# A fourth tile for the transposed values in the RWKV stage of a two-block fp32 network, paid for with unused DMA scratch

## The chip, the cores and the metric

The kernel runs as one launch on one core of a Trainium2 chip. The time is device microseconds of that core, the median of several executions. Smaller is better.

## What is computed

The program is a chain of two blocks over 256 tokens of width 1024, all in float32. The first has two layers, each a gated feed-forward, a mixer with a convolution and a linear recurrence, and another feed-forward. The second has an RWKV layer and a differential attention layer, over a context of 256 tokens and the 256 tokens themselves. The change lies in the RWKV layer. Cut to that, the reference is:

```python
def wkv_scan(r, w, k, v, kk, a, s0, reverse):
    def step(S, inp):
        r_t, w_t, k_t, v_t, kk_t, a_t = inp
        sa = jnp.einsum("bhvk,bhk->bhv", S, kk_t)
        S = (S * w_t[:, :, None, :] - sa[..., None] * (kk_t * a_t)[:, :, None, :]
             + v_t[..., None] * k_t[:, :, None, :])
        return S, jnp.einsum("bhvk,bhk->bhv", S, r_t)
    s_fin, o = lax.scan(step, s0, xs, reverse=reverse)

def rwkv7_mixer(...):            # 16 heads of 64
    oc_f, sc_f = scan_direction(con, 0, s0, False)   # context, forwards
    oc_b, sc_b = scan_direction(con, 1, s0, True)    # context, backwards
    ol_f, _ = scan_direction(lat, 0, sc_f, False)    # tokens, from the context's state
    ol_b, _ = scan_direction(lat, 1, sc_b, True)
    y = rwkv7_readout(ol_f + ol_b, lat, ...)
```

## The kernel before

A Python program writes out every engine's instructions in one fixed order. It keeps a clock of its own for each engine, with an assumed cost for each operation, and holds many generators ("chains"). At each matmul of the large products it lets those chains emit their next few instructions whose inputs and buffers its clock takes as ready. So a buffer that comes free earlier in that clock moves instructions on all five engines, and on the chip each engine then works through its own list strictly in that order.

The RWKV layer is done in eight pairs of heads, j = 0 to 7. For each pair:

- `rwkv` runs the large products with the weights `rw_in` (rows `ps<-ops,vhi` and `ps<-ops,vlo`, 128x512, called **fill** below, as are those of `rw_out` later). `prepare` works out decays and the tiles `q` on DVE, ACT and GpSimd.
- `products` is run for u = 0 (context) and u = 1 (tokens). It multiplies `q` by `q`, masks the results into a slot of `GE` (four slots, two of which lie in the tile `X`, so that rows say `GE` or `X`), transposes, and at its end takes one tile `uv` and copies the transposed values into it (ACT, `uv<-ps 64x512`).
- `inverse` starts when both u are through `products`. It inverts 32 small triangular systems: two large transposes on DVE (`invN<-GE` or `invN<-X`), a substitution in 30 operations on GpSimd (`invt`, `invX`), then small matmuls on PE (`ps<-invN,GE`, `ps<-GE,invN`, `ps<-invX,GE`) with DVE transposes and ACT copies between them. There is one set of work tiles.
- `recur` then goes through eight steps, four for u = 0 and four for u = 1. A step begins on PE with `ps<-S,q`, goes back and forth between PE and ACT or DVE (`rs`, `uv`), and, except for the last, ends with the update `S<-Sd,ps` on DVE. There is one state tile. At the end of each u it gives back that u's `GE` slot, its two `q` and its `uv`.

The numbers of tiles stand in one line, `NQ, NGE, NUV, NSH, NS, NPP = 8, 2, 3, 1, 9, 1`. The third of them is that of `uv`: `self.temps(rw, NUV, "uv", 512, "uv")`, each 512 x 4 bytes in every partition. `products` asks for one with

```python
uv, = yield from self.grab("uv")
```

which waits until one is free, and `recur` returns it with `self.give(z["uv"], kind="uv")`. `Bacc(...)` sets up the program; unless told otherwise it keeps 16384 bytes of every partition for descriptors of dynamic DMAs. Every transfer of this kernel is issued from SP.

Of the kernel before, what the change touches and what calls it, by code (L numbers as in the profile page):

```python
# [1031 lines left out]
HALF = [slice(64 * e, 64 * e + 64) for e in range(2)]  # L1032


NQ, NGE, NUV, NSH, NS, NPP = 8, 2, 3, 1, 9, 1
PACE, PACE_FROM = 0.0, 1
URGENT, RANKS = (1, 1, 1), (0, 0, 0, 0, 0)
NAQ = 12
# [1301 lines left out]
```

## Time and profile before

| | us |
|---|---|
| median of 3 runs | 2267.69 (2259.29 to 2274.60) |
| the profiled execution, its own time | 2270.05 |
| its span, first to last instruction | 2268.3 |
| TensorE busy / VectorE busy / ScalarE busy / GpSimd busy | 2076.7 / 1704.9 / 1251.4 / 862.3 |
| mean granted TensorE clock, as a share of 2.4 GHz | 0.925 |

Matmuls are pipelined and their ends are modelled, so a busy PE can hold waits inside a step. The granted clock is 1.0 or 0.5 at any moment; a figure between is a mean over a stretch. The recurrence of pair 0 begins at 1403 us of the span, and that of pair 7 has its last step at 2021 us.

### The profile page before, as it was taken

Reading aid. Unit: us, or ns where it says so; the run is one execution under the profiler, and the core shown is the slowest. Engines: PE = TensorE matmul, PEld = TensorE weight load, DVE = VectorE, ACT = ScalarE, POOL = GpSimd, SP = SyncE. Lnnn points to the kernel's source line nnn. Section 1 sums busy time; section 2 is a strip of 40 time slices with the busy share of each in tenths; the row PEclk is TensorE's granted clock in tenths of the full one; section 3 lists DMA queues with packets and bytes.
Section 4 is the critical chain, followed back from the end, with each engine's and each line's share of the span. In section 5 each row is a group of like instructions: output and inputs, shape, how many; then the busy total and the mean of one; then the engine's idle time right before and its main releaser. Section 6 shows DMA issues by size and latency. Waiting matters only on the chain.

```text
span 2268.3 us, 46757 instructions
## 1 busy us (share of the span) xinstructions
PE 2076.7 (92%) x18172; PEld 1878.2 (83%) x18172; DVE 1704.9 (75%) x2903; ACT 1251.4 (55%) x2802; POOL 862.3 (38%) x1092
## 2 busy tenths in 40 slices
PE   7988998998889889989999988999899889889998
PEld 7988988998889789989999966777677667667787
DVE  6689898888888888898666666675775773657896
ACT  6666585666666666765556554343344342336665
POOL 1144555344454453562001144543552542312231
PEclk9999999999999999999999997897887887869999
DMA  7666454666666565545656310010110110215442
GB/s 244 205 188 201 157 167 127 211 217 196 199 212 210 190 199 191 157 151 188 199 187 179 121 61 29 25 43 30 34 33 29 32 40 29 62 41 159 138 130 85
DMA packets 114095, 300.38 MB, mean 132 GB/s; under 512 B 12624, under 2 KB 18512, under 8 KB 113744
## 3 DMA queue, kind: packets, MB, share of 16 engines
q1 hardware_dynamic: 113872, 297.39, 41.4%
q8 instruction: 142, 2.33, 0.4%
q14 instruction: 81, 0.66, 0.1%
HBM read 292.89 MB, written 4.46 MB: 131 GB/s over the span
## 4 chain that ended last, share of the span: by engine, by line
PE 53%; DVE 21%; ACT 9%; issue 8%; POOL 5%; DMA 3%; SPq 0%; ACTq 0%; DVEq 0%; POOLq 0%
PE ps L89 53%; DVE wlo L89 8%; ACT ada L89 3%; DVE t L89 3%; ACT whi L89 3%; DVE b L89 2%; DMA adaw<-in_ada_w_dram 2%; POOL ada L89 2%; DVE X L89 1%; DVE q L89 1%; DVE invN L89 1%; DVE ops L89 1%; DVE GE L89 1%; POOL invt L89 1%; POOL invX L89 1%
## 5 line engine op out<-in xcount | busy, mean ns | idle before, releaser
L89 PE MATMUL ps<-ops,whi 128*128 128x256 f32 x4852 | 893.1, 282 | 18.3 <-ACT ops L89 9.1
L89 DVE TENSOR_TENSOR wlo<-wraw,whi 128x512 fp32r<-128x512 f32 (+2 forms) x792 | 675.8, 891 | 147.5 <-ACT whi L89 142.5
L89 PEld LDWEIGHTS ps<-ops,whi 128*128 128x128 f32 x4852 | 756.6, 190 | 22.2 <-ACT ops L89 9.3
L89 PE MATMUL ps<-ops,wlo 128*128 128x256 f32 x2504 | 709.1, 283 | 29.1 <-DVE wlo L89 28.7
L89 ACT ACTIVATE whi<-wraw 128x512 fp32r<-128x512 f32 (+2 forms) x798 | 437.7, 597 | 127.3 <-issue 59.2
L89 PEld LDWEIGHTS ps<-ops,wlo 128*128 128x128 f32 x2504 | 475.5, 190 | 37.1 <-DVE wlo L89 36.8
L89 PE MATMUL ps<-b,whi 128*128 128x256 f32 x1580 | 322.3, 290 | 31.9 <-ACT b L89 17.1
L89 POOL TENSOR_TENSOR ada<-adaw,ada 128x1024 f32<-128x1024 f32 x96 | 237.7, 2476 | 266.0 <-ACT ada L89 184.7
L89 PEld LDWEIGHTS ps<-b,whi 128*128 128x128 f32 x1580 | 261.8, 197 | 36.5 <-ACT b L89 17.9
L89 PE MATMUL ps<-ops,vhi 128*128 128x512 f32 (+1 forms) x624 | 227.4, 441 | 0.0
L89 PE MATMUL ps<-b,wlo 128*128 128x256 f32 x712 | 206.1, 290 | 8.9 <-DVE wlo L89 5.4
L89 DVE TENSOR_TENSOR vlo<-vraw,vhi 128x512 fp32r<-128x512 f32 x202 | 144.8, 731 | 24.5 <-ACT vhi L89 21.3
L89 POOL TENSOR_TENSOR sq<-sq,t 128x256 f32<-128x256 f32 x49 | 45.2, 922 | 279.3 <-ACT t L89 278.8
L89 POOL TENSOR_TENSOR small<-small,mhalf 128x8 f32<-128x8 f32 (+3 forms) x62 | 72.3, 1169 | 204.6 <-DVE small L89 202.1
L89 PEld LDWEIGHTS ps<-b,wlo 128*128 128x128 f32 x712 | 139.7, 196 | 12.2 <-DVE wlo L89 8.2
L89 ACT ACTIVATE ada<-ada 128x512 f32<-128x512 f32 (+1 forms) x193 | 120.6, 626 | 51.9 <-POOL ada L89 51.3
L89 PEld LDWEIGHTS ps<-ops,vhi 128*128 128x128 f32 x624 | 120.6, 206 | 25.7 <-issue 0.7
L89 ACT ACTIVATE vhi<-vraw 128x512 fp32r<-128x512 f32 x202 | 121.5, 619 | 28.9 <-PE ps L89 16.6
L89 PE MATMUL ps<-ops,vlo 128*128 128x512 f32 (+1 forms) x312 | 135.0, 433 | 0.2 <-DVE vlo L89 0.2
L89 PE MATMUL ps<-vhi,ops 128*128 128x512 f32 x384 | 127.7, 413 | 1.8 <-DVE ops L89 1.1
L89 POOL TENSOR_TENSOR Sd<-S,small 64x128 f32<-64x128 f32 x61 | 27.5, 451 | 196.5 <-DVE S L89 194.5
L89 ACT ACTIVATE b<-t 128x256 fp32r<-128x256 f32 (+1 forms) x104 | 42.4, 413 | 101.8 <-DVE t L89 101.7
(314 smaller groups left out, 3433.1 us busy)
## 6 DMA issues: line engine op xcount, KB each, us to landing
wraw<-in_ffn_w_up_dram SPq DMA_DIRECT2D x175, 512.0 KB, 3.9
wraw<-in_w_in_dram SPq DMA_DIRECT2D x80, 512.0 KB, 3.7
wraw<-in_ffn_w_down_dram SPq DMA_DIRECT2D x64, 512.0 KB, 3.6
adaw<-in_ada_w_dram SPq DMA_DIRECT2D x96, 256.0 KB, 4.0
vraw<-in_da_in_dram SPq DMA_DIRECT2D x96, 256.0 KB, 2.7
vraw<-in_rw_in_dram SPq DMA_DIRECT2D x60, 256.0 KB, 2.6
wraw<-in_ffn_w_down_dram SPq DMA_DIRECT2D x32, 384.0 KB, 3.8
wraw<-in_w_lru_up_dram SPq DMA_DIRECT2D x32, 320.0 KB, 2.9
```

The costliest lines, as they stand in the source:

```text
L89: return call(*args, **kw)
```

## The change

The third number of the line goes from 3 to 4: a fourth `uv` tile. For its 2048 bytes the scratch for dynamic DMAs is cut from the default to 1024 bytes, which moves the tiles to other addresses. No operation is added or taken away; the planner writes the same work in another order.

```diff
-NQ, NGE, NUV, NSH, NS, NPP = 8, 2, 3, 1, 9, 1
+NQ, NGE, NUV, NSH, NS, NPP = 8, 2, 4, 1, 9, 1
@@
-    nc = _bacc.Bacc("TRN2", target_bir_lowering=False, num_devices=1)
+    nc = _bacc.Bacc("TRN2", target_bir_lowering=False, num_devices=1, dynamic_dma_scratch_size=1024)
```

Up to the recurrence of pair 0 the orders differ in buffer numbers alone, and so they do, but for a few small products, behind the recurrence of pair 7. Between them two places show what moves.

DVE, recurrence of pair 0, where the inverse of pair 1 begins (`invN<-GE`). Before, the row at the top is the fourth update of the state, the last of u = 0:

```order
1404 L89 TENSOR_TENSOR S<-Sd,ps_89 64x2x64 x2
1405 L89 TENSOR_TENSOR ro_15858<-ro_15858,ps_92 64x128 x2
1406 L89 TENSOR_REDUCE small_73<-ro_15858 128x4
1407 L89 SCALAR_TENSOR_TENSOR ro_15858<-small_73,ro_15858 128x256
1408 L89 TENSOR_REDUCE small_73<-row_82 128x4
1409 L89 TENSOR_SCALAR small_73<-small_73 128x4
...
1413 L89 TENSOR_SCALAR uv_15849<-ps_92 64x2x64
1414 L89 STREAM_TRANSPOSE invN<-GE 32x1024
1415 L89 TENSOR_TENSOR S<-Sd,ps_95 64x2x64 x2
```

The same place now; the row at the top is the second update, and the last row the third:

```order
1392 L89 TENSOR_TENSOR S<-Sd,ps_90 64x2x64 x2
1393 L89 COPY ro_15859<-ps_92 64x128 x2
1394 L89 STREAM_TRANSPOSE invN<-GE 32x1024 x2
1395 L89 SCALAR_TENSOR_TENSOR w_15832<-s_15826,params,ps_95 128x512
1396 L89 TENSOR_SCALAR uv_15848<-ps_92 64x2x64
1397 L89 TENSOR_TENSOR w_15833<-w_15833,s_15826 128x512
1398 L89 SCALAR_TENSOR_TENSOR w_15835<-w_15835,w_15832 128x512
1399 L89 TENSOR_TENSOR S<-Sd,ps_89 64x2x64 x2
```

The inverse of pair 1 begins two steps earlier in the recurrence of pair 0.

PE, from the last step of pair 0 to the first of pair 1 (both begin with `ps<-S,q`). Before, the matmuls of the inverse of pair 1 all stand behind that last step:

```order
9221 L89 MATMUL ps_92<-S,q_15842 128x128 x2
...
9240 L89 MATMUL ps_94<-invN,GE 32x16 x64
...
9250 L89 MATMUL ps_94<-GE,invN 16x16 x64
...
9268 L89 MATMUL ps_95<-invX,GE 32x32 x16
...
9276 L89 MATMUL ps_95<-GE,invN 32x32 x16
...
9285 L89 MATMUL ps_93<-GE,invN 32x32 x16
...
9288 L89 MATMUL ps_92<-S,q_15844 128x128 x2
```

Now they stand inside the last three steps of pair 0; the rows are from the sixth step, the eighth, and the first of pair 1:

```order
9217 L89 MATMUL ps_92<-S,q_15842 128x128 x2
...
9220 L89 MATMUL ps_95<-invN,GE 32x16 x16
9221 L89 MATMUL ps_92<-rs,X 64x64 x4
9222 L89 MATMUL ps_95<-invN,GE 32x16 x32
...
9252 L89 MATMUL ps_92<-S,q_15842 128x128 x2
...
9255 L89 MATMUL ps_90<-invX,GE 32x32 x16
9256 L89 MATMUL ps_92<-rs,X 64x64 x4
9257 L89 MATMUL ps_89<-invX,GE 32x32 x16
...
9274 L89 MATMUL ps_89<-GE,invN 32x32 x16
...
9277 L89 MATMUL ps_92<-S,q_15844 128x128 x2
```

The stretch that held nothing of the recurrence is gone there, and the fill that stood in it is spread over the steps.

## Rows read from the trace of the kernel before

**Rows 1.** The page: granted clock in 40 slices, and the queue of the transfers.

```profile
PEclk9999999999999999999999997897887887869999
...
q1 hardware_dynamic: 113872, 297.39, 41.4%
```

**Rows 2.** Recurrences and gaps by turns: bounds, length, PE busy, clock, DMA share, GB/s.

```profile
1403.20:1448.00 44.80, 42.19 (x350) 0.89 0.11 36
1448.00:1476.30 28.30, 25.44 (x497) 0.88 0.09 31
1476.30:1525.20 48.90, 46.75 (x392) 0.97 0.13 44
1525.20:1559.00 33.80, 32.72 (x496) 0.69 0.06 18
1559.00:1616.90 57.90, 51.34 (x391) 0.86 0.14 42
1616.90:1649.40 32.50, 29.56 (x499) 0.81 0.08 27
1649.40:1698.10 48.70, 47.09 (x409) 0.92 0.12 39
1698.10:1727.70 29.60, 28.35 (x482) 0.74 0.08 24
1727.70:1781.70 54.00, 50.13 (x371) 0.89 0.12 38
1781.70:1816.30 34.60, 31.12 (x520) 0.80 0.07 21
1816.30:1861.90 45.60, 40.64 (x364) 0.89 0.16 50
1861.90:1895.30 33.40, 27.12 (x463) 0.56 0.01 1
1895.30:1948.80 53.50, 53.50 (x391) 0.93 0.19 60
1948.80:1976.20 27.40, 21.63 (x434) 0.67 0.10 25
1976.20:2021.10 44.90, 37.62 (x302) 0.63 0.10 34
```

**Rows 3.** DVE in order of time, end of u = 0 of pair 2.

```profile
1588.91 0.60 DVE L89 TENSOR_TENSOR S<-Sd,ps 64x128 f32<-64x128 f32 x2
...
1593.63 2.02 DVE L89 STREAM_TRANSPOSE invN<-GE 32x1024 f32<-32x1024 f32 x1
...
1596.26 1.89 DVE L89 STREAM_TRANSPOSE invN<-GE 32x1024 f32<-32x1024 f32 x1
```

**Rows 4.** ACT in order of time, the same place.

```profile
1592.15 0.59 ACT L89 ACTIVATE uv<-ps 64x512 f32<-64x512 f32 x1
```

**Rows 5.** PE in order of time, pair 2 and the gap before pair 3.

```profile
1600.30 1.19 PE L89 MATMUL ps<-S,q 128*128 128x128 f32 x4 [3.74 <-DVE S L89]
...
1616.87 0.61 PE L89 MATMUL ps<-S,q 128*128 128x128 f32 x4
...
1620.40 0.69 PE L89 MATMUL ps<-invN,GE 16*32 16x16 f32 x32
...
1629.98 0.19 PE L89 MATMUL ps<-GE,invN 32*16 32x16 f32 x2 [1.59 <-DVE GE L89]
...
1649.35 1.05 PE L89 MATMUL ps<-S,q 128*128 128x128 f32 x4
```

**Rows 6.** GpSimd's substitution, pairs 3 and 6 (PE, PEld, DVE, POOL busy); two equal operations.

```profile
1598.10:1616.10 18.00, 0.00 (x0) 0.00 (x0) 0.10 (x1) 12.85 (x30) 0.81 0.14 45
1851.60:1866.50 14.90, 0.00 (x0) 0.00 (x0) 0.12 (x1) 10.87 (x30) 0.97 0.00 1
...
1439.48 0.34 POOL L89 TENSOR_TENSOR invt<-invN,invX 64x96 f32<-64x96 f32 x1
...
1447.15 0.83 POOL L89 TENSOR_TENSOR invt<-invN,invX 64x96 f32<-64x96 f32 x1
```

## Prediction, made before the changed kernel ran

> **What bounds the kernel now.** I began with the slices of the page: the granted clock is at 9 tenths or more everywhere but in eleven of the twelve slices from 1361 to 2041 us, where it lies between 6 and 8 [rows 1]. That is the RWKV stage, and the change moves nothing outside it. I then cut this stage at the first and the last `ps<-S,q` of each pair and asked for PE's busy time and clock in each piece [rows 2]. It falls into two kinds of stretch by turns: the recurrence of a pair, from its first step to its last (seven steps, 44.8 to 57.9 us), and a **gap** from the last step of one pair to the first of the next (27.4 to 34.6 us). The eight recurrences take 398.3 us and the seven gaps 219.6 us, 617.9 us in all.
>
> What PE does in a stretch, put to full clock, is its busy time times its granted clock. In the gap after pair 2 that is 29.56 x 0.81 = 23.9 us of work in 32.5 us. Added up over the rows, the recurrences of pairs 0 to 6 hold 300.9 us of such work in 353.4 us, a filling of 0.85. The seven gaps hold 144.5 us in 219.6 us, a filling of 0.66, and pair 7's recurrence 23.7 us in 44.9 us. So the stage is bound neither by PE's work (469 us) nor by one long wait. It is a chain of latencies with fill between its links, and the gaps are where the fill is thinnest.
>
> Why there is a gap: the inverse of the next pair begins late. In pair 2 the fourth update of the state is at 1588.91, the second `uv` of pair 3 is written by ACT at 1592.15, and the first large transpose of pair 3's inverse begins on DVE at 1593.63 [rows 3, 4]. With three `uv` tiles the second `uv` of pair j + 1 has to wait for the first of pair j, which is returned after four steps. The inverse then takes until 1620.40 to reach PE and until 1649.35 to release the next recurrence, while the recurrence of pair 2 starts its last step at 1616.87 [rows 5]. So the inverse's first half hides under steps five to eight, and its second half is the gap.
>
> **The change, part by part.** The scratch costs nothing by the rows: 297 of the 300 MB that move go through one queue, hardware_dynamic [rows 1], all of it issued from SP and none from GpSimd, and no row shows a use of the scratch. What could be lost is only by the new addresses, which no row shows. From below and above I take 0, with 1403 us of unchanged order before the stage as the place where anything else would show.
>
> The fourth tile ends the wait for `uv`. What is late next is the products of the second half of pair j + 1, which need the `q` tiles and the `GE` slot that pair j - 1 gives back at its end. So the inverse can move from after the fourth step only to after the second or so. In the new order it begins after 2, 3, 2, 4, 2, 4 and 3 updates of pairs 0 to 6. This gives three kinds of passage:
>
> - Into pairs 1, 3 and 5 the inverse's matmuls stand inside the last three steps, and the gap is gone.
> - Into pairs 2 and 7 a part of them does.
> - Into pairs 4 and 6 all stand behind the last step as before. Those two gaps stay, at 29.6 and 33.4 us.
>
> The work in the gaps that go does not go: products, transposes, the inverse's own matmuls and fill are now in the steps. So I don't subtract gaps; I refill PE. The gaps that stay hold 21.0 + 15.2 = 36.2 us of work in 63.0 us. Pair 7's recurrence has nothing new to fill it and stays at 23.7 us in 44.9 us. The rest is 469.1 - 36.2 - 23.7 = 409.2 us of work, which now takes 617.9 - 63.0 - 44.9 = 510.0 us, a filling of 0.80. The question is the filling that this rest will have.
>
> The nearest rows are the recurrences. The two densest, pairs 1 and 6, reach 45.3 / 48.9 = 0.93 and 49.8 / 53.5 = 0.93; the mean of the seven is 0.85; the worst, pair 2, has 44.2 / 57.9 = 0.76 [rows 2]. So:
>
> - At 0.93 the rest takes 440 us, 70 less than now.
> - At 0.85 it takes 481 us, 29 less.
> - At 0.76 it takes 538 us, 28 more.
>
> I take 0.87. In the new order most steps hold 14 to 21 fill matmuls, as many as those of pair 6 now, which speaks for more than 0.85. Pair 5's steps are still thin, and into three pairs the DVE transposes of the inverse's second half (`GE<-invX`, which hold PE for 1.59 us in the gap [rows 5]) now stand between updates of the state. That speaks against 0.93. At 0.87 the rest takes 470.3 us, and **the saving is 39.7 us**.
>
> On the queues: PE, DVE, ACT and GpSimd are all in order, so each piece of the inverse that moves into the steps can now hold the recurrence behind it. On DVE that has a price in a row: at 1600.30 a step waited 3.74 us for the update of the state, which stood behind the two transposes of 2.02 and 1.89 us [rows 3, 5]. Such a wait is paid once a pair before; with the second half inside it could be paid twice in five pairs, 5 x 3.7 = 19 us, and 0.87 in place of 0.93 leaves 30 us for it. SP issues as many transfers as before, with a store of a finished pair a few loads earlier or later; the transfers use 1 to 19% of the DMA engines here [rows 2], so I cost that at nothing.
>
> **A rule on the port of GpSimd.** The substitution on GpSimd took 18.0 us in pair 3 and 14.9 us in pair 6, and of two equal operations one took 0.34 and the other 0.83 us [rows 6]. The Trainium skill ("SBUF — State Buffer", section "Who interferes with whom") says that a VectorE instruction with two inputs in SBUF and a GpSimd instruction that reads SBUF exclude each other, the second being held for the whole of the first. The uneven times agree with that, though no row shows which instruction held which. By that rule an inverse that begins amid the next pair's preparation meets more of DVE's two-input operations, and it is a mechanism of the third rival below.
>
> **The rivals.**
>
> *The gaps close as well as the order allows.* If the rest runs like pairs 1 and 6, it takes 440 us: 2270.05 - 70 = 2200 us for a profiled execution. For it speaks that a thin step now (pair 5, or the gaps at clocks of 0.56 and 0.69) loses half its speed, and the new order has fewer of these. Against it speaks that no recurrence with an inverse's second half in it exists in this trace.
>
> *The inverse inside the steps holds them up (slower).* PE reaches the moved matmuls before GpSimd or DVE is through, and since PE's list is strict, the recurrence behind them waits too, which the gap of before did not do to it. The inverse needs 1620.40 - 1593.63 = 26.8 us to reach PE and 29 us from there to the next pair; three steps are about 20 us (44.8 / 7 = 6.4 us each). Were the steps stretched to these times, each moved passage would lose up to 7 + 9 us of what it gained, the filling would be that of pair 2, 0.76, and the time 2270 + 28 = 2298 us. It decides from a filling under 0.80. Against it speaks that the gap holds 24 us of PE's work in its 32.5 us, much of it not the inverse's.
>
> *Nearly all is given back.* GpSimd's substitution at 18 us in place of 15 in five passages costs 15 us, and DVE's blocks 19 us; of 40 us little is left: 2255 to 2270 us.
>
> *The order does not do it on the chip.* The planner's clock is wrong by so much that PE waits for `uv` or `GE` elsewhere, and the stage is as long as now: 2270 us.
>
> **How the numbers follow.** The profiled execution took 2270.05 us, 2.4 us over the median of the runs, so the forecast is 2270.05 - 39.7 - 2.4 = **2228 us**. One per cent is 22.7 us; a measurement of this kernel, with runs from 2259 to 2275 us, can tell about that from no change. Chances: the forecast (a filling of 0.83 to 0.90, 2210 to 2250 us) 0.50; filled like pairs 1 and 6: 0.17; nearly all given back: 0.17; slower: 0.13; no effect: 0.03. Faster by over 1% is most of the first (those above 2245 us fall outside) and the second, 0.66; within 1% is 0.21; slower by over 1% is 0.13. The range runs from 2197 us, which is a filling of 0.93 throughout, to 2270 us, which takes in the third rival and leaves out the slower one and a little at the fast end.
>
> **What would show it.** In the profile of the changed kernel the last `ps<-S,q` of pairs 0, 2 and 4 and the first of the next should lie 7 to 12 us apart in place of 28 to 35, those of pairs 3 and 5 about 30 as now. The recurrences themselves should be longer, near 50 to 58 us. The mean clock between pair 0 and pair 7 should rise from 0.83 (the rows weighted by length) towards 0.88, and the stretches before 1403 us and after pair 7's last step keep their lengths, 1403 and 247 us. I am wrong if PE's waits for DVE and GpSimd inside the steps grow by more than 40 us, if the first 1403 us change, or if the gaps close and the recurrences grow by as much.

## The result, and the profile after

| | before | after |
|---|---|---|
| median, 4 runs each, us | 2271.14 (2259.29 to 2275.56) | 2235.49 (2230.19 to 2240.11) |
| ratio of the medians, with its 95% interval | | 0.9865 [0.9833, 0.9897] |
| the profiled execution, own time / span, us | 2270.05 / 2268.3 | 2239.28 / 2237.3 |
| span up to pair 0's first step / RWKV stage / behind it, us | 1403.2 / 617.9 / 247.2 | 1399.4 / 587.1 / 250.8 |

The change takes 35.6 us off the medians, against 39.7 us forecast. In two of the kernels below some runs were in a slow state (two of ten, and one of six), and medians and ratios leave these out. Of the 31.0 us between the two spans, 30.8 us lie in the stage between pair 0's first step and pair 7's last. The stretch ahead of it is 3.8 us shorter, with the same order but for buffer numbers, and that behind it 3.6 us longer. Both lie within what one order does from execution to execution: nine kernels of the table below have this order up to pair 0's first step, and reach it at 1395.4 to 1403.2 us; and the order of before, run with the smaller scratch, takes 250.7 us behind the stage.

The page after, busy times, clock and queue (for [rows 1]):

```profile
PE 2064.5 (92%) x18172; PEld 1872.4 (84%) x18172; DVE 1720.8 (77%) x2915; ACT 1250.3 (56%) x2801; POOL 877.2 (39%) x1081
...
PEclk9999999999999999999999997998998977859999
...
q1 hardware_dynamic: 113872, 297.39, 42.4%
```

The packets and bytes are the same. PE has as many instructions and is busy 12 us less. The operations are as many in all, but the planner also chooses the engine of some: VectorE has 12 more, GpSimd 11 and ScalarE 1 fewer. In the stage it is eleven of the 110 `Sd<-S,small` (the decay of the state) that went from GpSimd to VectorE. Of the twelve slices of the stage its clock rose in six and fell in two, the last of which, at 5, is now the lowest.

Recurrences and gaps of the changed kernel by turns, with the columns of [rows 2]:

```profile
1399.40:1453.90 54.50, 52.83 (x631) 0.91 0.15 45
1453.90:1467.40 13.50, 13.50 (x182) 0.75 0.07 22
1467.40:1528.10 60.70, 55.69 (x581) 0.97 0.11 36
1528.10:1555.80 27.70, 25.31 (x364) 0.75 0.09 30
1555.80:1609.90 54.10, 50.80 (x625) 0.91 0.09 26
1609.90:1622.00 12.10, 11.11 (x184) 1.00 0.23 67
1622.00:1674.20 52.20, 50.47 (x426) 0.93 0.11 37
1674.20:1709.10 34.90, 31.52 (x515) 0.80 0.10 32
1709.10:1763.60 54.50, 52.90 (x701) 0.97 0.10 31
1763.60:1772.70 9.10, 9.10 (x107) 0.83 0.22 75
1772.70:1821.60 48.90, 44.76 (x411) 0.92 0.17 52
1821.60:1858.40 36.80, 31.02 (x480) 0.55 0.03 9
1858.40:1913.80 55.40, 54.10 (x555) 0.91 0.13 39
1913.80:1931.90 18.10, 18.07 (x281) 0.81 0.18 60
1931.90:1986.50 54.60, 46.56 (x322) 0.61 0.13 39
```

Read the second column of every second row. The gaps behind pairs 0, 2 and 4 are 13.5, 12.1 and 9.1 us in place of 28 to 35, and those behind pairs 1 and 6 fell from 33.8 to 27.7 and from 27.4 to 18.1. Those behind pairs 3 and 5 rose to 34.9 and 36.8. In all the gaps went from 219.6 to 152.2 us, and the recurrences from 398.3 to 434.9: of 67.4 us closed, 36.6 came back as longer recurrences. Busy time times clock, added over the rows, gives 470.0 us of PE's work, against 469.1 before. The work is the same to 0.2%, and PE gets through it sooner. (Over all fourteen kernels below, which run the same matmuls in the stage, this sum goes from about 461 to 470 us, so it holds to 2%.)

What the fourth tile does is seen in pair 0. ACT of the changed kernel in order of time:

```profile
1409.48 0.59 ACT L89 ACTIVATE uv<-ps 64x512 f32<-64x512 f32 x1
```

DVE of the changed kernel, the same place:

```profile
1404.03 0.60 DVE L89 TENSOR_TENSOR S<-Sd,ps 64x128 f32<-64x128 f32 x2 [0.54 <-PE ps L89]
...
1409.71 0.60 DVE L89 TENSOR_TENSOR S<-Sd,ps 64x128 f32<-64x128 f32 x2
...
1410.86 3.98 DVE L89 STREAM_TRANSPOSE invN<-GE 32x1024 f32<-32x1024 f32 x2
```

The second `uv` of pair 1 is written at 1409.48, while pair 0 is at its second update of the state (1409.71), and the inverse begins 1.4 us later. Before, this came behind the fourth update, as the rows of pair 2 show [rows 3, 4].

PE of the changed kernel, pair 2's last steps and the passage into pair 3 (for [rows 5]):

```profile
1588.32 0.61 PE L89 MATMUL ps<-S,q 128*128 128x128 f32 x4
...
1590.83 1.19 PE L89 MATMUL ps<-invN,GE 16*32 16x16 f32 x64
...
1599.22 0.60 PE L89 MATMUL ps<-GE,invN 32*16 32x16 f32 x30 [1.91 <-DVE GE L89]
...
1611.03 1.19 PE L89 MATMUL ps<-invX,GE 32*32 32x32 f32 x32
...
1621.95 0.71 PE L89 MATMUL ps<-S,q 128*128 128x128 f32 x4 [0.99 <-POOL S L89]
```

The `invN,GE` products that opened the gap at 1620.40 now stand among the steps of pair 2 (its last begins at 1609.89), and only the end of the inverse is left behind it.

### The profile page after: what moved, and what is told of

It reads as the page before. It is cut to its first block, busy times and chain, and to the rows that moved or that the text cites. A ratio compares the mean times of both kernels' runs of the same rounds, so it can differ in the third digit from the quotient of the medians.

```text
span 2237.3 us, 46733 instructions
## 1 busy us (share of the span) xinstructions
PE 2064.5 (92%) x18172; PEld 1872.4 (84%) x18172; DVE 1720.8 (77%) x2915; ACT 1250.3 (56%) x2801; POOL 877.2 (39%) x1081
## 4 chain that ended last, share of the span: by engine, by line
PE 52%; DVE 22%; ACT 9%; issue 8%; POOL 7%; DMA 3%; SPq 0%; DVEq 0%; ACTq 0%; POOLq 0%
PE ps L89 52%; DVE wlo L89 8%; ACT ada L89 3%; DVE t L89 3%; ACT whi L89 2%; DVE b L89 2%; POOL invt L89 2%; POOL invX L89 2%; DMA adaw<-in_ada_w_dram 1%; POOL ada L89 1%; DVE invN L89 1%; DVE X L89 1%; DVE ops L89 1%; DVE vlo L89 1%; ACT b L89 1%
## 5 line engine op out<-in xcount | busy, mean ns | idle before, releaser
L89 PE MATMUL ps<-ops,wlo 128*128 128x256 f32 x2504 | 710.0, 284 | 27.5 <-DVE wlo L89 27.4
L89 DVE TENSOR_TENSOR vlo<-vraw,vhi 128x512 fp32r<-128x512 f32 x202 | 150.0, 757 | 25.3 <-ACT vhi L89 22.7
L89 PEld LDWEIGHTS ps<-ops,vhi 128*128 128x128 f32 x624 | 121.5, 207 | 26.9 <-DVE ops L89 1.2
L89 ACT ACTIVATE b<-t 128x256 fp32r<-128x256 f32 (+1 forms) x104 | 42.3, 412 | 104.9 <-DVE t L89 104.9
L89 PEld LDWEIGHTS ps<-vhi,ops 128*128 128x128 f32 x384 | 72.2, 195 | 19.6 <-DVE ops L89 2.3
```

Of the source, the lines that this page charges most:

```text
L89: return call(*args, **kw)
```

## The experiments

Three theories at the start. **A**: the gain comes from the earlier inverse, passage by passage. **B**: it comes from the room itself, by other addresses or the smaller scratch. **C**: it is luck of the planner, and any reordering moves the time as much. All ratios are to the kernel before, run on the same chip. "Starts" is the number of state updates that the pair ahead has done when the inverse of pairs 1 to 7 begins. The quoted expectations use letters of their own for their rivals. The stage and the stretch behind it are of one profiled execution for each kernel, while the runs of one kernel lie 9 to 30 us apart, so a few us between two stages say nothing.

| kernel | starts | median, us | ratio [95%] | stage, us | behind the stage, us |
|---|---|---|---|---|---|
| before | 4 4 4 4 4 4 4 | (ratio 1) | | 617.9 | 247.2 |
| after | 2 3 2 4 2 4 3 | 2235.49 | 0.9865 [0.9833, 0.9897] | 587.1 | 250.8 |
| smaller scratch alone | 4 4 4 4 4 4 4 | 2265.44 | 1.0008 [0.9994, 1.0023] | 617.7 | 250.7 |
| four `uv`, inverse held | 4 4 4 4 4 4 4 | 2270.67 | 1.0034 [1.0019, 1.0049] | 615.6 | 252.1 |
| held for pairs up to 3 | 4 4 4 2 3 3 3 | 2229.74 | 0.9852 [0.9825, 0.9879] | 588.7 | 237.8 |
| held for pairs 4 to 7 | 2 3 2 4 4 4 4 | 2240.25 | 0.9903 [0.9877, 0.9928] | 601.9 | 238.0 |
| four `uv`, ten `q` | 2 3 2 2 3 3 3 | 2225.90 | 0.9826 [0.9778, 0.9873] | 585.7 | 237.8 |
| three `uv`, ten `q` | 4 4 4 4 4 5 4 | 2269.57 | 1.0020 [0.9992, 1.0048] | 614.2 | 244.4 |
| before, delay 236 | 4 4 4 4 4 4 4 | 2256.72 | 0.9965 [0.9936, 0.9994] | 606.3 | 243.5 |
| after, delay 236 | 2 4 3 2 3 2 4 | 2224.74 | 0.9805 [0.9753, 0.9857] | 581.3 | 250.4 |
| held to the third step | 3 3 3 3 3 3 3 | 2244.95 | 0.9896 [0.9862, 0.9930] | 602.5 | 241.4 |
| ten `q`, delay 236 | 2 3 2 4 2 3 3 | 2222.84 | 0.9816 [0.9761, 0.9871] | 584.9 | 246.8 |
| before, delay 244 | 4 4 4 4 4 4 4 | 2278.61 | 1.0041 [1.0010, 1.0072] | 631.2 | 247.8 |
| after, delay 244 | 2 3 2 3 1 4 2 | 2217.37 | 0.9786 [0.9745, 0.9827] | 575.6 | 244.7 |

**The scratch alone**: the changed kernel with three `uv`, so the order of before with the scratch of after.

```diff
-NQ, NGE, NUV, NSH, NS, NPP = 8, 2, 4, 1, 9, 1
+NQ, NGE, NUV, NSH, NS, NPP = 8, 2, 3, 1, 9, 1
```

> Three uv tiles as before, only the DMA scratch cut to 1024 bytes: every engine's list is word for word that of before, and the tiles lie at other addresses. My theory (the gain is the earlier inverse alone): ratio to before 0.995 to 1.005. Rival A (the addresses or the scratch give the gain, or part of it): 0.985 to 0.992.

Measured 1.0008, and a stage of 617.7 us beside 617.9. The scratch and the addresses cost and give nothing that these runs can tell, and B falls.

**Four tiles, but the inverse held back**: it waits in the planner until the pair ahead has ended its u = 0, as it did before. The tile is there, and `uv` is written as early as in the changed kernel.

```diff
 def inverse(self, j, units, pc, bv, sg):
+        while True and self.halved < j:
+            yield
         work, = yield from self.grab("inv")
...
 @@ recur, at the end of each u
+            if u == 0:
+                self.halved = j + 1
             self.give(z["slot"], kind=z["slot"][0])
```

> Four uv tiles, but the inverse of pair j may not begin before the recurrence of pair j-1 has ended its first half, as it was before; in the order it begins after 4 updates in all seven passages. My theory: the gaps of 27 to 35 us are back in all seven passages and the ratio to before is 0.99 to 1.005. Rival B (the room for the second uv is what helps, the products done earlier and out of the gap, whenever the inverse begins): 0.98 to 0.99.

ACT of this kernel, in order of time, pair 0:

```profile
1405.52 0.59 ACT L89 ACTIVATE uv<-ps 64x512 f32<-64x512 f32 x1
```

DVE of this kernel, the same pair:

```profile
1419.42 0.60 DVE L89 TENSOR_TENSOR S<-Sd,ps 64x128 f32<-64x128 f32 x2 [0.97 <-PE ps L89]
...
1421.37 3.97 DVE L89 STREAM_TRANSPOSE invN<-GE 32x1024 f32<-32x1024 f32 x2
```

Its first pair and gap, in the columns of [rows 2]:

```profile
1395.40:1442.00 46.60, 46.33 (x386) 1.00 0.19 57
1442.00:1476.70 34.70, 27.77 (x497) 0.66 0.03 10
```

The second `uv` lies ready 15 us before the inverse begins, and all seven gaps are back at 26.9 to 38.0 us. The ratio is 1.0034: the whole gain is gone. So it is the start of the inverse that gains, and an earlier `uv` copy by itself nothing. A stands in its main part. The order is not that of before in all else: the planner put the fill into the recurrences (87 to 94 such matmuls in each of the first five, at a mean clock of 1.00, for 57 to 80 before) and left 0 to 14 in each of the gaps behind them, which run at 0.59 to 0.67. Denser recurrences alone gain nothing either.

**One half of the passages each**: the same wait only for pairs up to 3 (`while j < 4 and ...`), and only for pairs 4 to 7 (`while j >= 4 and ...`).

> As the kernel with the wait for the first half, but only for the inverses of pairs 1 to 3; those of pairs 4 to 7 begin after 2, 3, 3 and 3 updates. My theory (each passage gives its own share): gaps of about 30 us into pairs 1 to 3, shorter ones into 4 to 7, ratio 0.989 to 0.996. Rival C (the gain lies in one place, or is luck of the whole order): 0.985 or 1.0.

> The other half: the inverses of pairs 4 to 7 are held to the fourth update, those of pairs 1 to 3 begin after 2, 3 and 2 as in the change. My theory: gaps of 13, 28 and 12 us into pairs 1 to 3, about 30 us into 4 to 7, ratio 0.989 to 0.995, and the savings of the two halves add up to about the 31 to 36 us of the change. Rival C: 0.985 or 1.0, with sums that don't add.

The stage gains 29.2 us with the late passages alone and 16.0 us with the early ones alone, which together is 45, where the change itself has 30.8. The shares don't add, so that part of A falls. From pair 3's first step to the end of the stage, the kernel with late passages alone takes 343.1 us, the changed one 364.5 us. Recurrences and gaps of pairs 3 and 4, in the kernel with late passages alone:

```profile
1648.60:1706.00 57.40, 54.08 (x711) 0.94 0.14 43
1706.00:1712.70 6.70, 6.70 (x114) 1.00 0.01 2
1712.70:1772.00 59.30, 54.19 (x631) 0.91 0.09 28
1772.00:1791.60 19.60, 19.60 (x262) 0.83 0.13 42
```

Its gaps behind pairs 3 and 4 are 6.7 and 19.6 us, those of the changed kernel 34.9 and 9.1. Two things differ. Holding the early passages gave the planner other starts later: 2, 3, 3, 3 into pairs 4 to 7 where the changed kernel has 4, 2, 4, 3. And the first three pairs of the changed kernel take 222.6 us in place of the 246.2 of before, but with 188.5 us of work in place of 195.9, so that more work (281.5 us against 273.2) is left for the rest. What that costs is seen in the kernel with the early passages alone, which is the changed kernel up to pair 4: it gains the same 23.6 us there, and from pair 3's first step on takes 379.3 us where before took 371.7, both with starts of 4. So 7.6 us are given back, and this is in its 16.0 already. The 14 us that are missing go with the later starts: behind the same early pairs, 4, 2, 4, 3 take 364.5 us for 379.3, which is 15 us, while 2, 3, 3, 3 take 343.1 us where before took 371.7, which is 29. The expectation for the late passages alone was missed: the ratio, 0.9852, is its rival's 0.985.

**More `q` tiles**: the prediction named `q` and `GE` as what is late next. With ten `q` and four `uv`, and with ten `q` and three `uv`:

```diff
-NQ, NGE, NUV, NSH, NS, NPP = 8, 2, 4, 1, 9, 1
+NQ, NGE, NUV, NSH, NS, NPP = 10, 2, 4, 1, 9, 1
```

> The change with ten q tiles in place of eight (they fit into the freed scratch too). In the order the inverses begin after 2, 3, 2, 2, 3, 3 and 3 updates in place of 2, 3, 2, 4, 2, 4, 3. My theory (with uv free, the tiles that the pair before last gives back are the next limit, and they are why every second passage stays late): no passage keeps a gap of 35 us, ratio 0.975 to 0.985, a further 0 to 20 us under the change. Rival D (PE's filling is the limit now, the gaps that stay are made up elsewhere): 0.985 to 0.991, as the change.

> Ten q tiles, but three uv as before: the inverses begin after 4 (once 5) updates. My theory: uv is the limit that comes first, so more q alone does nothing, ratio 0.995 to 1.005. Rival (any more room early in the chain helps): 0.985 to 0.993.

Ten `q` alone do nothing for the start (4 to 5 updates, ratio 1.002). On top of the fourth `uv` they bring the inverse of pairs 4 and 6 forward to 2 and 3 updates: `uv` is the first limit, `q` the second. Yet closing these two gaps takes only 1.4 us off the stage, for others grew: those behind pairs 2, 4 and 6 are 22.1, 26.8 and 25.7 us where the changed kernel has 12.1, 9.1 and 18.1. Rows of the kernel with ten `q`: recurrence of pair 3 and the gap behind it, then the gap behind pair 5.

```profile
1623.40:1691.00 67.60, 62.12 (x698) 0.87 0.11 36
1691.00:1702.60 11.60, 10.71 (x195) 1.00 0.01 4
...
1839.10:1857.50 18.40, 18.12 (x238) 0.50 0.01 2
```

The gap behind pair 3 fell from 34.9 to 11.6 us, and the recurrence in front of it rose from 52.2 to 67.6. The one behind pair 5 halved, and runs at a clock of 0.50. No gap of 35 us is left, as expected, but whether the time follows is not shown: the interval of the ratio reaches from the expectation into its rival's range, and overlaps that of the changed kernel. In the profiled executions the stretch behind the stage is shorter too, 237.8 us in place of 250.8, as in the two half-held kernels (237.8 and 238.0).

**How much is luck of the order.** The planner adds a delay, 240 in both kernels, to the end of each operation before what follows may count on it. With 236 and 244 it writes other orders of the same work; both kernels were run with both.

```diff
-GAP2 = 240
+GAP2 = 236     # and 244
```

> The kernel before with the planner's assumed delay between engines at 236 in place of 240 ns: three uv, the same operations in another order, inverses after 4 updates as before. It measures what an unrelated reordering does. My theory: 0.993 to 1.007. Rival C (the gain of the change is of the size of any reordering): beyond 0.99 or 1.01.

> The change with the planner's assumed delay at 236 ns: inverses after 2, 4, 3, 2, 3, 2 and 4 updates, so other passages stay late than in the change. My theory: the gain is there again, 0.980 to 0.992 of before and at least 18 us under the kernel before with the same delay. Rival C: 0.995 to 1.005.

> The kernel before with the planner's assumed delay at 244 ns: third order of three uv, all inverses after 4 updates. My theory: 0.99 to 1.01, and 18 us or more over the change at 244 ns. Rival C: within 8 us of it.

> The change with the planner's assumed delay at 244 ns: inverses after 2, 3, 2, 3, 1, 4 and 2 updates. Third order of four uv. My theory: 0.977 to 0.992. Rival C (luck of the order): no better than the kernel before at 244 ns.

The order alone moves the kernel before by -0.35% to +0.41%. The fourth tile gains 32.0 us at 236, 35.6 at 240 and 61.2 at 244, three times the larger of these shifts or more, so C falls as the cause of the gain. The whole table says the same: the five ratios of other kernels whose inverses begin after four updates (one of them once after five) are 0.9965 to 1.0041, the eight with earlier starts 0.9786 to 0.9903. One other thing goes with the starts. In the kernels of the first kind 49 to 56 of the 110 `Sd<-S,small` are on VectorE, in those of the second 59 to 72. That this is the gain is not borne out: in the kernel before no update of the state waited for an `Sd` on GpSimd, and its waits were for PE (22.9 us) and ScalarE's `w` (1.8 us). But the order sets the size of the gain: the starts at 244 are 2 3 2 3 1 4 2, and this has the lowest ratio measured, 0.9786 (its interval overlaps those of the three next: four tiles at 236, and ten `q` with either delay). Its stage and that of the kernel before with the same delay, all engines (length, then PE, PEld, DVE, ACT, POOL busy, clock, DMA share, GB/s), before first:

```profile
1397.90:2029.10 631.20, 570.24 (x6344) 449.44 (x6343) 385.25 (x722) 238.87 (x536) 254.43 (x457) 0.82 0.12 35
```

```profile
1398.10:1973.80 575.70, 542.72 (x6345) 429.87 (x6343) 397.43 (x738) 236.71 (x534) 259.43 (x442) 0.86 0.13 38
```

**The same start everywhere, and both additions together.** In the first, the inverse waits until the pair ahead has done three steps; in the second there are ten `q` and a delay of 236.

```diff
 def inverse(self, j, units, pc, bv, sg):
+        while self.steps < 8 * (j - 1) + 3:
+            yield
...
 @@ recur, behind each step
+                self.steps = 8 * j + 4 * u + s + 1
```

> The change, with the inverse of pair j held until three steps of the recurrence of pair j-1 are written out: in the order all seven inverses begin after exactly 3 updates, in place of 2, 3, 2, 4, 2, 4, 3. Theory F (the stage is held by how densely PE can be filled, not by single gaps): gaps of some 15 to 25 us in all passages, the stage again 582 to 592 us between the first and the last step, ratio 0.978 to 0.99. Rival G (the two gaps of 35 and 37 us that the change leaves cost what they last over a step, some 25 us each): stage under 575 us, ratio under 0.975.

> Four uv, ten q and the planner's assumed delay at 236 ns: the two edits that were each a little under the change. Inverses after 2, 3, 2, 4, 2, 3 and 3 updates. Theory F: stage 580 to 590 us, the rest of the span by the luck of the order behind it, ratio 0.975 to 0.988. Rival: they add, under 0.972.

An even start after three updates gives gaps of 18.3 to 29.1 us and a stage of 602.5 us, 15.4 us more than the uneven starts of the changed kernel. Neither theory had that: F expected 582 to 592 us, G under 575. Ten `q` and a delay of 236 give a ratio of 0.9816, beside 0.9826 and 0.9805 with either alone, and the rival's 0.972 lies outside its interval: no sign that they add.

## Why the prediction was right, and where it was off

- **The direction and the mechanism** held. The inverse moved into the steps, the gaps closed where the order closes them, the work stayed (470.0 against 469.1 us), and undoing the earlier start alone undid the whole gain.
- **The filling of the rest** held: 399.3 us of work in 460.8 us is 0.867, for 0.87 taken and 0.80 before. That it came out so near is luck, for two of the reasons given for it did not hold. "Most steps hold 14 to 21 fill matmuls" is true in the trace of 22 of 56 steps, for 18 before: the recurrences of pairs 0 to 6 hold 522 fill matmuls, for 510, and what moved into them is 1120 matmuls of the inverse, where there were none. And the waits on DVE, which were to keep it under 0.93, did not come. Of the 61.5 us that the rest is not filled, 22.2 are idle time of PE and 39.3 the lower clock; before they were 37.9 and 62.9 of 100.8.
- **The stretches said to stay** are the term that was mis-sized. The gaps into pairs 4 and 6 took 71.7 us for 63.0, and pair 7's recurrence 54.6 us for 44.9, 18.4 us more in all. They did not hold still because other work came into them: these three hold 42.3 + 28.4 us of work, 10.8 more than assumed, at the same filling (0.56). The rest holds 399.3 for 409.2, which gives back 9.5 us (460.8 us for 470.3 forecast). The fill is where it shows. The stage has 696 fill matmuls in both kernels. Those alone, PE's busy time and count, in the gaps into pairs 4 and 6 and in pair 7's recurrence, before and then after:

```profile
1698.10:1727.70 29.60, 9.73 (x22) 0.74 0.08 24
1861.90:1895.30 33.40, 3.15 (x6) 0.56 0.01 1
1976.20:2021.10 44.90, 7.17 (x31) 0.63 0.10 34
```

```profile
1674.20:1709.10 34.90, 12.15 (x35) 0.80 0.10 32
1821.60:1858.40 36.80, 7.37 (x15) 0.55 0.03 9
1931.90:1986.50 54.60, 15.77 (x48) 0.61 0.13 39
```

  So "pair 7's recurrence has nothing new to fill it" was wrong, 48 fill matmuls for 31, and the new order had it to be counted. Part of these 18.4 us can be the execution: with the order of before and the smaller scratch, pair 7's recurrence took 52.0 us at a clock of 0.50, and the three together 110.4 us for 107.9. The stage so gained 30.8 us and not 39.7. The median came out at 2235.5 us for 2228; 3.4 us of that are that the median before rose from 2267.69 to 2271.14 with a fourth run.
- **The gaps** were to be 7 to 12 us and were 13.5, 12.1 and 9.1; those said to be about 30 were 34.9 and 36.8. The recurrences were to be 50 to 58 us, and six of eight were; pair 1's was 60.7 and pair 5's 48.9. The stage's clock was to go from 0.83 towards 0.88; it went from 0.82 to 0.85 by the windows of the whole stage.
- **The waits on DVE** were priced at 19 us, and did not come. PE's waits in the stage of the changed kernel (total us, times, longest):

```profile
PE ps L89 <- DVE S L89: 3.9, 3, 3.3
...
PE ps L89 <- DVE GE L89: 2.8, 3, 1.9
```

  Before, PE waited 10.2 us there for `S`, in six waits, and 8.0 for `GE`. So the 3.74 us of [rows 5] was the longest of six and not the price of every pair, and the 19 us were too many from the start. Such a wait came once more, at 3.3 us. Why the others went no run isolates.
- **The rivals.** "The gaps close as well as the order allows" would have needed a filling of 0.93; the rest reached 0.867. "The inverse inside the steps holds them up" decides below 0.80, and the changed kernel is above it. "Nearly all is given back" saw the size of one thing and not its cause or effect: GpSimd's substitution, from its first operation to its last, took 122.7 us over the seven inverses in place of 108.6, 14 us where 15 was priced. But with the inverse held it took 121.9 us, so this length does not need the early start, and PE's waits for GpSimd did not grow by it (for `ro` they fell from 5.7 to 3.2 us). "The order does not do it on the chip" is out.
- **The signs of being wrong.** Of the three, "if the first 1403 us change" came by the letter, with 1399.4 us; kernels with the same order up to there have 1395.4 to 1403.2, so 3.8 us say nothing.

Where PE's time went in the stage: idle 52.7 us before and 39.4 after, which is 13 us, and busy time lost to the lower clock level about 96 and 78 us, which is 18. By this account more than half of the gain is busy time that had been spent at the lower clock level.

Two things stay open in part. The stretch behind the stage is 238 us in three kernels and 247 to 252 in six others (five lie between). Its order differs: in the first 60 us of it the kernel with the late passages alone ran 257 matmuls at a mean clock of 0.91, the changed one 220 at 0.79. No run isolates that. And the gap behind pair 5 runs at a clock of 0.50 to 0.60 in ten of the fourteen kernels. Nearly nothing is transferred there in these ten (a DMA share of 0.01 to 0.03), and it holds 0 to 15 fill matmuls, where the other gaps of before hold 18 to 31. Whether more fill would mend it was not tried.

## What to carry to other kernels

Where a long in-order chain has fill between its links, count PE's work (busy time times granted clock) by stretch, and forecast with its sum held fixed: what leaves a stretch must turn up in another, the stretches "that stay" among them, and where it turns up can be counted from the new order before it runs. One more buffer is worth what it lets start earlier, so read from the trace which operation the freed wait lets begin; holding that one operation back with the buffer in place is the experiment that shows it. When a planner writes the order, rerun both kernels at two or three values of some harmless parameter before a gain under 1% is believed.

## What the runs showed of the hardware

The same operations took longer because of where they stood. VectorE in the stage by operation and shape, before, after, and with the inverse held (count, busy us, mean ns, then the idle time ahead):

```profile
L89 DVE TENSOR_TENSOR S<-Sd,ps 64x128 f32<-64x128 f32 x112 | 31.9, 285 | 26.9 <-PE ps L89 22.9 <-ACT w L89 1.8
L89 DVE TENSOR_TENSOR Sd<-S,small 64x128 f32<-64x128 f32 x50 | 20.2, 405 | 1.1
```

```profile
L89 DVE TENSOR_TENSOR S<-Sd,ps 64x128 f32<-64x128 f32 x112 | 31.9, 284 | 32.2 <-PE ps L89 30.0
L89 DVE TENSOR_TENSOR Sd<-S,small 64x128 f32<-64x128 f32 x61 | 31.7, 520 | 2.0 <-POOL S L89 0.8
```

```profile
L89 DVE TENSOR_TENSOR S<-Sd,ps 64x128 f32<-64x128 f32 x112 | 31.9, 285 | 25.1 <-PE ps L89 21.2 <-issue 1.5
L89 DVE TENSOR_TENSOR Sd<-S,small 64x128 f32<-64x128 f32 x56 | 22.4, 400 | 1.1
```

The two rows have one shape. `S<-Sd,ps` reads one input from PSUM and takes 285, 284 and 285 ns. `Sd<-S,small` reads both from SBUF and takes 405, 520 and 400 ns on the mean, and its longest in the changed kernel took 2546 ns. Each one over 350 ns (18 of 50, 33 of 61 and 24 of 56) has GpSimd at work beside it for some of its time, though some 15 of the shorter ones in each kernel have too. The longest, in order of time on VectorE and GpSimd:

```profile
1481.26 3.03 POOL L89 TENSOR_TENSOR q<-q,small 128x512 f32<-128x512 f32 x3
...
1481.89 2.55 DVE L89 TENSOR_TENSOR Sd<-S,small 64x128 f32<-64x128 f32 x1
```

It begins amid the first of three GpSimd operations of 1.03 us, back to back, and ends 0.15 us behind the third, at 1484.44: one operation, of a shape whose shortest took 272 ns, was held over all three. GpSimd's substitution, `invt` alone in the stage (length of the window, busy time and count), after and with the inverse held:

```profile
1395.00:2011.00 616.00, 96.71 (x210) 0.84 0.13 39
```

```profile
1395.00:2011.00 616.00, 86.66 (x210) 0.81 0.11 35
```

Before it was 87.38 us for the same 210 operations. With the inverse put back, these busy times are back too, so it is the company that stretches both. The Trainium skill ("SBUF — State Buffer", section "Who interferes with whom") has GpSimd and a VectorE operation with two SBUF inputs lock each other out; that the PSUM form kept its 285 ns while the SBUF form grew by 28% agrees with it. In all, the stage held 17.5 us more of VectorE's busy time and 9.8 us more of GpSimd's than before. Not all of the first is stretch: of the 11.5 us that `Sd<-S,small` grew, some 4.5 are the eleven operations that came from GpSimd (at 405 ns each). PE's waits for the two engines did not grow: for VectorE they fell from 31.4 to 25.9 us, for GpSimd from 8.9 to 4.2.
